# Two chained transformer blocks on one core: other order of the first loads, and planner costs of instructions fitted to a trace

## Chip, cores and metric

One core of one Trainium2 chip. The metric is the device time of one execution in microseconds (us): the kernel before takes 3340.11 us, the median of 3 runs (3338.27 to 3342.55).

## The reference, cut to what matters

The input x is 512 tokens by 1024 features in fp32. Two blocks of depth two follow each other:

```python
# first block
x = x + even_mixer(rmsnorm(x))       # gated linear attention (GLA), 4 heads, and differential attention, 4 heads
x = x + conv_ffn(rmsnorm(x))         # 1024 -> 2 x 2816 -> 1024, causal convolution of 3
x = x + odd_mixer(rmsnorm(x))        # dilated attention, 3 patterns
x = x + conv_ffn(rmsnorm(x))
# second block, for i in (0, 1); cs is a context of 256 tokens, needed for i == 0 only
m = silu(c) @ w_mod[i] + b_mod[i]    # 9 x 1024 modulation values, w_mod is 1024 x 9216; likewise from c_ctx
x = x + 0.5 * m2 * swiglu(modulate(x, m0, m1))
x = x + m5 * mixer(modulate(x, m3, m4))   # i == 0: attention of 8 query heads on 2 key heads, and pooling; i == 1: gated mixing
x = x + 0.5 * m8 * swiglu(modulate(x, m6, m7))
```

In the even mixer the eight head outputs are normed (the GLA heads are also multiplied by silu of a gate), joined to 1024 features and multiplied by `w_out`.

## The kernel before

**Numbers.** Every large product is done as three matmuls of a rounded fp32 type (hi·hi, hi·lo, lo·hi; `mm3`). Activations stand as pairs: `hh`, `hl` for a normed input, `mh`, `ml` for the middle tiles that go into an output projection. A weight block of 128 rows by 1024 columns (512 KB, `raw`) comes by one DMA, mostly from SP's queue (`wdma`), and is split into `whi` on ACT and `wlo` on DVE, each in two halves of 512.

**Stages.** They run one after the other: a0 (even mixer), b0 (FFN), a1 (odd mixer), b1, c0 (half FFN, with the context), d0 (attention and pooling), e0, c1, d1, e1. Tokens are worked on in one piece of 512 columns, or in two halves of 256 at the first and the last projection of a stage (`passes`), so that the next norm can begin on the first half.

**The order.** Each engine runs its instructions in program order. The program order is made when the kernel is built: small steps of a stage (a head's scores, its norm, a softmax) are generators, called tasks, and after every `mm3` the method `tick` may step some of them. It asks a planner: `Clock` keeps a modelled time for each engine, `Clock.cost` gives the duration it assumes for an instruction, and a task is stepped when its inputs are due by the modelled time of TensorE. Only the first `width` tasks whose predecessors are done are looked at (4 in a0 and a1, 8 in d0). The same model decides when weights are split ahead (`wahead`) and when a step of `mod_task` is taken. So a change of a number in `Clock.cost` reorders instructions in the whole program, on all engines, while the work stays what it is.

**a0's end.** The projection out of the mixer is in two parts. `proj_out` takes the four heads of the differential attention, 96 matmuls of 512 columns into tiles `gm`, while the GLA runs: decays (`la` on PE, `lae` on ACT, `lc` on DVE), running sums (`cum`, `cul`), scores (`attp`), states (`kv`), outputs (`oa`). Then `o_norm` norms the head outputs: a square on ACT (`osq`), a sum over the features on PE (`ss`), on DVE `hv`, on ACT a logarithm and an exponential (`rb`), on DVE five operations of 512 columns (two write `osq`, three write `rb`), then `mh` on ACT and `ml` on DVE. `final` multiplies the four GLA heads by their part of `w_out`, 256 columns at a time. The gates need silu (`sg`), which stands in another table of ACT than the logarithm and the exponential, so a change between them is an `ACT_TABLE_LOAD`.

**d0's attention.** 16 units (`attn_unit`): eight score matmuls into three PSUM tiles (`as1` twice 512 columns, `as0` 2 x 256), row maxima on DVE (`amx`, `nb`), four exponentials with sums on ACT (`ap1`, `ap0`), twelve transposes on PE (`at`), copies (`aw`), 25 matmuls with the values (`apo`), and a scaling (`arb`, `ao`).

**The modulation.** `mod_task` multiplies `w_mod` by silu(c) row block by row block on DVE, into sums `macc`, with 512 KB loads `rawm`; its steps are spread over a0 to c0.

**Recording.** In the profile every instruction of the engines carries line 172, that of the wrapper that records it. Tile names with a number behind (`gm_2828`) are single buffers; the trace leaves the number out.

Of the kernel before, what the change touches and what calls it, by code (L numbers as in the profile page):

```python
# [9 lines left out]
F32 = mybir.dt.float32  # L10
# [5 lines left out]
OP = mybir.AluOpType  # L16
# [12 lines left out]
NG = 66  # L29
# [68 lines left out]
class Clock:  # L98
# [18 lines left out]
    def cost(self, engine, op, out, ins, extra):  # L117
        n = 1
        for x in (out if op != "tensor_reduce" else ins[0]).shape[1:]:
            n *= x  # L120
        if engine == "tensor":
            if op == "transpose":
                return 0.11
            dt = ins[-1].dtype
            if dt == F32:
                return max(0.213, n / 600)
            return n / 2400 if dt == BF16 or n >= 256 else n / 600
        if op == "dma_start":
            return 0.06
        psum = any(x.space == PSUM for x in ins)  # L130
        if engine == "vector":
            scalars = op in ("tensor_scalar", "scalar_tensor_tensor")
            each = 0.00052 if op == "tensor_scalar" and not psum else 0.00833 if op == "reciprocal" else 0.00104
            return (0.13 if scalars else 0.07) + 0.03 * psum + each * n
        if engine == "scalar":
            return 0.1 + 0.00083 * n + 0.05 * sum(len(x.shape) == 2 and x.shape[1] == 1 for x in ins[1:]) + extra
        return 0.1 + 0.0023 * n

    def issue(self, engine, op, args, kwargs):
# [5 lines left out]
        end = start + self.cost(engine, op, out, ins, 0.24 * ("accum_out" in kwargs))  # L145
# [36 lines left out]
class Kern:  # L182
    def __init__(self, tc, ctx, a, out, dump=None, plan=None):
# [701 lines left out]
    def mod_task(self):  # L885
        nc = self.nc
        parts = [(i, u, k0) for i in range(2) for u in range(36) for k0 in range(0, NK, KU)]
        raws = []

        def load(j):  # L890
            if j < len(parts):
                i, u, k0 = parts[j]
                raw = self.wp.tile([P, KU, 256], F32, tag="rawm", name="rawm", bufs=MB)
                nc.sync.dma_start(raw, self.a["w_mod"][i, u, :, k0:k0 + KU])
                raws.append(raw)
# [3 lines left out]
        rows = [self.sp.tile([P, 96], F32, tag="mrow", name="mrow", bufs=3) for _ in range(2)]  # L899
# [11 lines left out]
        for j, (i, u, k0) in enumerate(parts):  # L911
            if k0 == 0:
                todo = [(self.sc, self.mT[i])]
                if i == 0 and u < 20:
                    todo.append((self.scc, self.mcT))
                accs = [self.wp.tile([P, 256], F32, tag="macc", name="macc", bufs=2) for _ in todo]
# [12 lines left out]
            if k0 + KU == NK:  # L929
                x = u % 12  # L930
                for acc, r in zip(accs, rows):
                    nc.vector.transpose(tr := self.wp.tile([P, 256], F32, tag="mtr", name="mtr", bufs=1), acc)
                    nc.vector.tensor_reduce(r[:, 8 * x:8 * x + 8], tr.rearrange("p (b c) -> p b c", c=32),
                                            axis=AX.X, op=OP.add)
                last = len(todo) == 2 and u == 19
                if x == 11 or last:
                    yield
                    for (_, m), r in list(zip(todo, rows))[1 if last else 0:]:
                        sums(i, m, r, u - x, x + 1)
                    if x == 11:  # L940
                        self.mod_done = 36 * i + u
                        rows = [self.sp.tile([P, 96], F32, tag="mrow", name="mrow", bufs=3) for _ in range(2)]
                yield
# [610 lines left out]
    def attn_unit(self, t, c, qs, kk, va, ao):  # L1554
# [257 lines left out]
def lay_out(inputs):  # L1812
# [4 lines left out]
    def blocks(w, cols=None):  # L1817
# [4 lines left out]
        return con(w.reshape(k // P, P, m // 256, 256).transpose(2, 1, 0, 3))  # L1822
# [27 lines left out]
    d["w_mod"] = np.stack([blocks(x) for x in f("w_mod_2")])  # L1850
# [79 lines left out]
```

## Time and profile before

| what | value |
|---|---|
| median of 3 runs | 3340.11 us |
| the profiled execution | 3336.78 us, its span 3335.0 us |
| PE (TensorE) busy | 3290.2 us, 99% |
| PEld (weight loads of PE) busy | 2874.7 us, 86% |
| DVE (VectorE) busy | 2101.9 us, 63% |
| ACT (ScalarE) busy | 1237.7 us, 37% |
| DMA | 355.73 MB, mean 107 GB/s |

PE is busy nearly all the time, so what it waits for, and where, says more than the shares do. A row of the timeline has start, duration, engine, line, operation, output<-inputs, shapes and count, and in brackets the idle time before and what ended it. A row of the waits has the engine and what it was about to run, whom it waited for, microseconds in total, times and the longest. The clock of PE has two levels, 1.2 and 2.4 GHz, written as 0.50 and 1.00 in the windows.

### The profile page before, as it was taken

The page shows a single profiled execution, that of the slowest core. Times are in us where ns is not written, and L with a number is a line of the kernel's source. Part 1 is how long each engine was busy: PE and PEld are TensorE (multiplying, and loading weights), DVE is VectorE, ACT ScalarE, POOL GpSimd, SP SyncE. Part 2 cuts the span into 40 slices and gives each one's busy share as a digit, 9 for nine tenths or more (in the row PEclk, how much of TensorE's full clock was granted, in tenths as well). Part 3 has the DMA queues.
Part 4 walks back from the last instruction along what each step waited for, and adds up shares of the span by engine and source line. Part 5 has one row for each costly group of instructions (what it writes and reads, how often), then busy time and mean ns, then how long its engine had stood idle before and what let it go on. Part 6 is the DMA issues. An engine that isn't in the chain of part 4 may idle for free.

```text
span 3335.0 us, 48346 instructions
## 1 busy us (share of the span) xinstructions
PE 3290.2 (99%) x19172; PEld 2874.7 (86%) x19172; DVE 2101.9 (63%) x4577; ACT 1237.7 (37%) x2515; POOL 5.2 (0%) x13
## 2 busy tenths in 40 slices
PE   8999999999999999999999989999999999999999
PEld 7789888988998889888888977988898889998888
DVE  6868988857498878655555776855663335463333
ACT  4544434364443434212222465322332233442231
POOL 0000000000000000000000000000000000000000
PEclk9999999999999999999999999999999999999999
DMA  3223444322134443443333301445522233232232
GB/s 120 70 64 105 150 125 137 122 65 76 58 114 145 127 133 107 142 146 119 112 118 126 96 24 51 148 137 158 160 93 82 95 103 99 87 98 91 92 101 70
DMA packets 105814, 355.73 MB, mean 107 GB/s; under 512 B 12642, under 2 KB 18931, under 8 KB 105587
## 3 DMA queue, kind: packets, MB, share of 16 engines
q1 hardware_dynamic: 105154, 351.98, 33.5%
q8 instruction: 150, 2.46, 0.3%
q14 instruction: 78, 0.63, 0.1%
q10 hardware_dynamic: 432, 0.66, 0.1%
HBM read 350.50 MB, written 2.10 MB: 106 GB/s over the span
## 4 chain that ended last, share of the span: by engine, by line
PE 90%; DVE 7%; ACT 2%; issue 1%; DMA 1%; SPq 0%; DVEq 0%; ACTq 0%
PE gm L172 81%; PE gt L172 4%; ACT ap L172 1%; DVE wlo L172 1%; PE ss L172 1%; DVE nt L172 1%; DVE amx L172 1%; DVE x L172 0%; PE os L172 0%; PE opo L172 0%; DVE rb L172 0%; DVE rs_t L172 0%; DVE nsq L172 0%; PE qst L172 0%; DVE hl L172 0%
## 5 line engine op out<-in xcount | busy, mean ns | idle before, releaser
L172 PE MATMUL gm<-hh,whi 128*128 128x512 f32 (+1 forms) x2872 | 1040.4, 362 | 6.9 <-ACT whi L172 6.9
L172 PE MATMUL gm<-hl,whi 128*128 128x512 f32 (+1 forms) x2872 | 1033.9, 360 | 5.6 <-DVE hl L172 5.6
L172 PE MATMUL gm<-hh,wlo 128*128 128x512 f32 (+1 forms) x2872 | 1031.5, 359 | 5.1 <-DVE wlo L172 5.1
L172 DVE TENSOR_TENSOR wlo<-raw,whi 128x512 fp32r<-128x512 f32 (+1 forms) x1028 | 662.1, 681 | 77.2 <-ACT whi L172 75.2
L172 ACT ACTIVATE whi<-raw 128x512 fp32r<-128x512 f32 (+1 forms) x1028 | 582.4, 617 | 296.6 <-DMA raw<-in_ffn_w_dram 106.5
L172 PEld LDWEIGHTS gm<-hh,wlo 128*128 128x128 f32 x2872 | 543.7, 189 | 88.5 <-DVE wlo L172 5.9
L172 PEld LDWEIGHTS gm<-hh,whi 128*128 128x128 f32 x2872 | 544.6, 190 | 74.0 <-ACT whi L172 6.9
L172 PEld LDWEIGHTS gm<-hl,whi 128*128 128x128 f32 x2872 | 544.5, 190 | 72.9 <-DVE hl L172 6.6
L172 PE MATMUL gm<-mh,whi 128*128 128x512 f32 (+1 forms) x1696 | 576.6, 340 | 0.0
L172 PE MATMUL gm<-ml,whi 128*128 128x512 f32 (+1 forms) x1696 | 573.0, 338 | 0.8 <-DVE ml L172 0.8
L172 PE MATMUL gm<-mh,wlo 128*128 128x512 f32 (+1 forms) x1696 | 571.7, 337 | 0.0
L172 DVE TENSOR_TENSOR ga<-ga,gm 128x512 f32<-128x512 f32 (+1 forms) x110 | 68.0, 633 | 497.7 <-PE gm L172 328.2
L172 PEld LDWEIGHTS gm<-mh,wlo 128*128 128x128 f32 x1696 | 321.8, 190 | 34.7
L172 PEld LDWEIGHTS gm<-ml,whi 128*128 128x128 f32 x1696 | 322.2, 190 | 29.1 <-DVE ml L172 1.0
L172 PEld LDWEIGHTS gm<-mh,whi 128*128 128x128 f32 x1696 | 322.2, 190 | 28.9 <-issue 0.9
L172 ACT ACTIVATE ga<-gm 128x512 f32<-128x512 f32 (+1 forms) x110 | 58.8, 554 | 716.6 <-PE gm L172 716.6
L172 DVE SCALAR_TENSOR_TENSOR macc<-rawm,sc,macc 128x256 f32<-128x256 f32 x504 | 244.0, 484 | 15.4
L172 DVE SCALAR_TENSOR_TENSOR x<-gm,modt,x 128x256 f32<-128x256 f32 (+1 forms) x184 | 105.9, 607 | 226.4 <-PE gm L172 226.3
L172 PEld LDWEIGHTS gm<-hc,whi 128*128 128x128 f32 x736 | 135.0, 188 | 29.0 <-ACT whi L172 1.6
L172 DVE SCALAR_TENSOR_TENSOR cy<-gm,vec,cy 128x511 f32<-128x511 f32 (+1 forms) x176 | 127.7, 746 | 45.9 <-ACT cy L172 42.8
L172 PE MATMUL gm<-hc,whi 128*128 128x256 f32 x736 | 145.1, 281 | 1.3 <-ACT whi L172 1.3
L172 ACT ACTIVATE nsq<-x 128x256 f32<-128x256 f32 x160 | 60.2, 414 | 176.8 <-DVE x L172 176.7
(314 smaller groups left out, 3425.6 us busy)
## 6 DMA issues: line engine op xcount, KB each, us to landing
raw<-in_ffn_w_dram SPq DMA_DIRECT2D x256, 512.0 KB, 4.4
rawm<-in_w_mod_dram SPq DMA_DIRECT2D x144, 512.0 KB, 4.4
raw<-in_ffn_w_up_dram SPq DMA_DIRECT2D x88, 512.0 KB, 3.8
raw<-in_ffn_w_down_dram SPq DMA_DIRECT2D x40, 512.0 KB, 3.7
raw<-in_od_w_in_dram SPq DMA_DIRECT2D x36, 512.0 KB, 3.8
raw<-in_ev_w_in_dram SPq DMA_DIRECT2D x23, 512.0 KB, 3.7
raw<-in_w_in_c_dram SPq DMA_DIRECT2D x16, 512.0 KB, 4.3
raw<-in_w_in_a_dram SPq DMA_DIRECT2D x10, 512.0 KB, 4.4
```

The source lines that it names most:

```text
L172: return f(*args, **kwargs)
```

## The change

Three things are edited.

- The first loads: of the four first weight blocks one more is issued ahead of the second half of x on SP's queue, and one goes to ACT's queue, ahead of the constants.
- `Clock.cost` gets other numbers for matmuls, DVE and ACT; `NG`, the number of 2 KB work tiles per partition, goes from 66 to 64.
- Two pieces of work are cut differently. `mod_task` takes 1024 columns with one DVE instruction (144 parts, of 512 KB each as before) in the place of four of 256. `attn_unit` does all row maxima of a unit first, three reductions and two small operations, and then the four exponentials; before, each half had its maxima and then its exponentials.

The core of the diff:

```diff
-NG = 66
+NG = 64
...
-            dt = ins[-1].dtype
-            if dt == F32:
-                return max(0.213, n / 600)
-            return n / 2400 if dt == BF16 or n >= 256 else n / 600
+            if ins[-1].dtype == F32:
+                rows, cols = ins[0].shape[0], ins[0].shape[-1]
+                return max(0.214, n / 597) * (0.6 if rows <= 64 or cols <= 64 else 1.0)
+            return (n + 32) / 2400 if n >= 256 else 0.066
...
-            scalars = op in ("tensor_scalar", "scalar_tensor_tensor")
-            each = 0.00052 if op == "tensor_scalar" and not psum else 0.00833 if op == "reciprocal" else 0.00104
-            return (0.13 if scalars else 0.07) + 0.03 * psum + each * n
+            fast = not psum and op in ("tensor_scalar", "tensor_copy")
+            each = 0.00052 if fast else 0.00833 if op == "reciprocal" else 0.00104
+            return 0.155 + 0.06 * (scalars > 0) + each * n
         if engine == "scalar":
-            return 0.1 + 0.00083 * n + 0.05 * sum(len(x.shape) == 2 and x.shape[1] == 1 for x in ins[1:]) + extra
+            return 0.2 + 0.00083 * n + 0.075 * scalars + extra
...
-            self.wdma()
+            self.wdma()
+            self.wdma(nc.scalar)
+            self.wdma()
         load(0, 4, 1)
         nc.scalar.dma_start(self.cst[:, :256], a["cst"][:, :256])
         load(4, 8, 1)
-        if plan is not None:
-            for _ in range(2):
-                self.wdma()
...
-                for k in range(KU):
-                    sk = s[:, k0 + k:k0 + k + 1]
-                    if k0 + k == 0:
-                        nc.vector.tensor_scalar(acc, raw[:, k], sk, None, op0=OP.mult)
-                    else:
-                        nc.vector.scalar_tensor_tensor(acc, raw[:, k], sk, acc, op0=OP.mult, op1=OP.add)
+                sk = s[:, k:k + 1]
+                if k == 0:
+                    nc.vector.tensor_scalar(acc, raw, sk, None, op0=OP.mult)
+                else:
+                    nc.vector.scalar_tensor_tensor(acc, raw, sk, acc, op0=OP.mult, op1=OP.add)
...
+        for j in range(2):
+            nc.vector.tensor_reduce(mx[:, j:j + 1], s1[j], axis=AX.X, op=OP.max)
+        nc.vector.tensor_reduce(mx[:, 2:4], s0.rearrange("p (j k) -> p j k", j=2), axis=AX.X, op=OP.max)
+        nc.vector.tensor_tensor(nb, mx[:, 0:2], mx[:, 2:4], op=OP.max)
+        nc.vector.tensor_mul(nb, nb, neg[:, 2 * t:2 * t + 2])
         for j in range(2):
             k, half, cc = slice(j, j + 1), slice(j * C, (j + 1) * C), slice(2 * t + j, 2 * t + j + 1)
-            nc.vector.tensor_reduce(mx[:, k], s1[j], axis=AX.X, op=OP.max)
-            nc.vector.tensor_reduce(mx[:, 2 + j:3 + j], s0[:, half], axis=AX.X, op=OP.max)
-            nc.vector.scalar_tensor_tensor(nb[:, k], mx[:, k], mx[:, 2 + j:3 + j], neg[:, cc], op0=OP.max, op1=OP.mult)
```

The counts of instructions: PE has the same 18483 matmuls and transposes before and after, in another order; DVE goes from 4574 to 4006; ACT has 14 table loads in the place of 10, the four new ones in a0.

**Where the order moves.** A row is an instruction as the program has it, with its tiles. Line 172 of the kernel before is line 173 of the changed one.

SP's queue at the start of the program, before (`raw` are weight blocks, `x` the input; the second block of weights is `raw_84` in both):

```order
L172 DMA raw_84<-in_ev_w_in_dram 128x1024
L172 DMA x_75<-in_xT_dram 128x4x256 x2
L172 DMA raw_89<-in_ev_w_in_dram 128x1024
L172 DMA raw_91<-in_ev_w_in_dram 128x1024
L172 DMA vec_77<-in_vec_dram 128x600
L172 DMA cst_76<-in_cst_dram 128x1042
```

and after, where the third block, `raw_86`, has gone to ACT's queue, just behind the first:

```order
L173 DMA raw_84<-in_ev_w_in_dram 128x1024
L173 DMA raw_88<-in_ev_w_in_dram 128x1024
L173 DMA x_75<-in_xT_dram 128x4x256 x2
L173 DMA vec_77<-in_vec_dram 128x600
L173 DMA cst_76<-in_cst_dram 128x1042
L173 DMA raw_128<-in_ev_w_in_dram 128x1024
```

Two blocks stand ahead of the second half of x (`128x4x256`) on SP, and one on ACT, where one stood on SP and none on ACT beside the first.

PE at a0's end, before: the four sums `ss` of the GLA heads' norms, and what stands behind them. `mh_1692`, `mh_1976` are heads of the differential attention, long done; 81 such rows of `proj_out` follow the last `ss` before the first row of `final`, which reads `mh_2665`, the first GLA head:

```order
L172 MATMUL ss_2632<-osq_2615,cst_76 128x512
L172 MATMUL ss_2639<-osq_2617,cst_76 128x512
L172 MATMUL ss_2646<-osq_2619,cst_76 128x512
L172 MATMUL ss_2653<-osq_2621,cst_76 128x512
L172 MATMUL gm_2624<-mh_1692,whi_2228 128x512
L172 MATMUL gm_2624<-ml_1693,whi_2228 128x512
L172 MATMUL gm_2624<-mh_1692,wlo_2229 128x512
```

and after: `mh_2796` and `ml_2797` are the first GLA head, so these are the rows of `final`, right behind the last `ss`; all 96 matmuls of `proj_out` stand further up, between the steps of the GLA:

```order
L173 MATMUL ss_2763<-osq_2755,cst_76 128x512
L173 MATMUL ss_2770<-osq_2757,cst_76 128x512
L173 MATMUL ss_2777<-osq_2759,cst_76 128x512
L173 MATMUL ss_2784<-osq_2761,cst_76 128x512
L173 MATMUL gm_2828<-mh_2796,whi_2405 128x256
L173 MATMUL gm_2828<-ml_2797,whi_2405 128x256
L173 MATMUL gm_2828<-mh_2796,wlo_2406 128x256
```

On DVE, `ml_2797` comes after the five operations of all four heads, as `ml_2666` does in the kernel before.

ACT in the last third of a0, before: the decays of the second pair of GLA heads (`lae_2083`), and the square `osq_2125` of the last head of the differential attention; the gates `sg` come 20 rows later:

```order
L172 ACTIVATE lae_2083<-la_2079 128x512
L172 ACTIVATE lae_2083<-lae_2083 128x512 x2
L172 ACTIVATE dor_1119<-po_2088 128x128
L172 ACTIVATE whi_2109<-raw_1783 128x512
L172 ACTIVATE osq_2125<-dor_1119 128x512
L172 ACTIVATE rb_2131<-hv_2129 128x512
L172 ACTIVATE rb_2131<-rb_2131 128x512
```

and after: the decays of the first pair (`lae_2293`), the gates of two heads, the same head's square (here `osq_2331`), with three table loads between them:

```order
L173 ACT_TABLE_LOAD
L173 ACTIVATE lae_2293<-lae_2293 128x512
L173 ACTIVATE dor_1113<-po_2305 128x128
L173 ACT_TABLE_LOAD
L173 ACTIVATE sg_2320<-sg_2320 128x512
L173 ACTIVATE sg_2323<-sg_2323 128x512
L173 ACT_TABLE_LOAD
L173 ACTIVATE osq_2331<-dor_1113 128x512
L173 ACTIVATE rb_2337<-hv_2335 128x512
L173 ACTIVATE rb_2337<-rb_2337 128x512
```

PE's sum over that head is `ss_2333<-osq_2331`; the matmuls ahead of it on PE are those of `gm_2195` and `gm_2196`, which the gates `sg_2320` and `sg_2323` are made from. Behind `ss_2333` stand the second `la`, nine matmuls of `proj_out` for three heads of the differential attention, and then one that reads `mh_2354`, this same head.

DVE in one of the last units of d0's attention, before:

```order
L172 TENSOR_REDUCE amx_20773<-as1_20763 128x1
L172 TENSOR_REDUCE amx_20773<-as0_20762 128x1
L172 SCALAR_TENSOR_TENSOR nb_20774<-amx_20773,neg_20205 128x1
L172 TENSOR_REDUCE amx_20773<-as1_20764 128x1
L172 TENSOR_REDUCE amx_20773<-as0_20762 128x1
L172 SCALAR_TENSOR_TENSOR nb_20774<-amx_20773,neg_20205 128x1
```

and after, one unit:

```order
L173 TENSOR_REDUCE amx_20160<-as1_20150 128x1
L173 TENSOR_REDUCE amx_20160<-as1_20151 128x1
L173 TENSOR_REDUCE amx_20160<-as0_20149 128x2
L173 TENSOR_TENSOR nb_20161<-amx_20160 128x2
L173 TENSOR_TENSOR nb_20161<-nb_20161,neg_19626 128x2
```

The second half's maxima no longer stand behind those of the first half. On PE, no projection matmul stands between the scores of the last nine units in the changed program; before, 69 matmuls of 512 columns stand there.

## Rows read from the trace of the kernel before

**Rows 1.** The page's head: span, and busy time of the engines.

```profile
span 3335.0 us, 48346 instructions
PE 3290.2 (99%) x19172; PEld 2874.7 (86%) x19172; DVE 2101.9 (63%) x4577; ACT 1237.7 (37%) x2515; POOL 5.2 (0%) x13
```

**Rows 2.** Windows: us from:to, length, busy time by engine, PE clock, DMA.

```profile
16.68:21.30 4.62, 4.62 (x21) 4.62 (x22) 4.62 (x10) 4.62 (x12) 2.20 (x4) 0.50 0.64 201
...
1938.00:2067.00 129.00, 113.98 (x902) 95.08 (x901) 90.26 (x246) 80.43 (x208) 0.00 (x0) 0.97 0.12 40
1979.40:1984.00 4.60, 4.49 (x22) 4.49 (x23) 3.65 (x12) 1.24 (x3) 0.00 (x0) 0.51 0.00 0
```

**Rows 3.** Timeline of the start: ACT, DVE and PE around PE's longest early wait.

```profile
14.06 0.63 ACT L172 ACTIVATE whi<-raw 128x512 fp32r<-128x512 f32 x1 [1.66 <-DMA raw<-in_ev_w_in_dram]
...
15.33 0.69 DVE L172 TENSOR_TENSOR nsq<-nsq 128x512 f32<-128x512 f32 x1 [3.03 <-ACT nsq L172]
...
16.68 0.58 PE L172 MATMUL gm<-hh,wlo 128*128 128x256 f32 x1 [4.41 <-DVE wlo L172]
```

**Rows 4.** Timeline of a0's end, PE and DVE: last `ss` to `final`.

```profile
233.41 0.79 PE L172 MATMUL gm<-mh,whi 128*128 128x512 f32 x1
...
234.62 0.68 DVE L172 TENSOR_TENSOR osq<-rb 128x512 f32<-128x512 f32 x1
...
238.79 0.68 DVE L172 TENSOR_TENSOR osq<-rb 128x512 f32<-128x512 f32 x1
...
249.42 0.75 DVE L172 SCALAR_TENSOR_TENSOR rb<-rb,vec,sg 128x512 f32<-128x512 f32 x1
...
250.69 0.68 DVE L172 TENSOR_TENSOR ml<-rb,mh 128x512 fp32r<-128x512 f32 x1
...
252.22 0.28 PE L172 MATMUL gm<-mh,whi 128*128 128x256 f32 x1
```

**Rows 5.** Timeline of ACT in a0: decays, table loads, gates.

```profile
168.31 1.29 ACT L172 ACTIVATE lae<-lae 128x512 f32<-128x512 f32 x2
...
199.90 1.28 ACT L172 ACT_TABLE_LOAD   x1
201.24 1.23 ACT L172 ACTIVATE sg<-sg 128x512 f32<-128x512 f32 x2
...
250.86 1.28 ACT L172 ACT_TABLE_LOAD   x1
252.15 1.15 ACT L172 ACTIVATE whi<-raw 128x512 fp32r<-128x512 f32 x2
```

**Rows 6.** Timeline of one head's norm in a0, DVE's five operations: first and last.

```profile
162.15 0.68 DVE L172 TENSOR_TENSOR osq<-rb 128x512 f32<-128x512 f32 x1
...
165.04 0.49 DVE L172 TENSOR_SCALAR rb<-rb,vec 128x512 f32<-128x512 f32 x1
```

**Rows 7.** Waits of PE from 90 to 300 us, a0's second half and b0's start.

```profile
PE gm L172 <- DVE hl L172: 3.4, 2, 1.9
PE gm L172 <- DVE ml L172: 0.8, 1, 0.8
```

**Rows 8.** Waits of PE from 1935 to 2070 us, d0's attention: the longest.

```profile
PE qst L172 <- ACT qsq L172: 6.5, 1, 6.5
```

**Rows 9.** Groups by shape, 1938 to 2067 us: maxima on DVE, exponentials on ACT.

```profile
L172 ACT ACTIVATE ap<-as,nb,cc 128x512 f32<-128x512 f32 x32 | 24.9, 778 | 34.9 <-DVE nb L172 34.9
...
L172 DVE TENSOR_REDUCE amx<-as 128x1 f32<-128x512 f32 x32 | 21.9, 683 | 0.6 <-PE as L172 0.6
...
L172 ACT ACTIVATE ap<-as,nb,cc 128x256 f32<-128x256 f32 x32 | 17.8, 555 | 0.0
L172 ACT ACTIVATE aw<-at 128x512 f32<-128x512 f32 x32 | 17.4, 607 | 3.9 <-PE at L172 3.9
...
L172 DVE TENSOR_REDUCE amx<-as 128x1 f32<-128x256 f32 x32 | 13.4, 420 | 18.2 <-ACT ap L172 17.9 <-PE as L172 0.2
```

**Rows 10.** Timeline of PE in the attention: one unit's value products and transposes.

```profile
1951.30 1.53 PE L172 MATMUL apo<-aw,va 128*64 128x128 f32 x24
1952.76 1.53 PE L172 MATMUL at<-cst,ap 128*128 128x128 f32 x12
```

**Rows 11.** Groups by shape, 40 to 2200 us: the modulation's products on DVE.

```profile
L172 DVE SCALAR_TENSOR_TENSOR macc<-rawm,sc,macc 128x256 f32<-128x256 f32 x423 | 204.8, 484 | 13.0
```

More of the change, by code (lines that the diff above doesn't have):

```diff
@@ L130, in cost @@
         psum = any(x.space == PSUM for x in ins)
+        scalars = sum(len(x.shape) == 2 and x.shape[1] == 1 for x in ins[1:])
         if engine == "vector":
-            scalars = op in ("tensor_scalar", "scalar_tensor_tensor")
-            each = 0.00052 if op == "tensor_scalar" and not psum else 0.00833 if op == "reciprocal" else 0.00104
-            return (0.13 if scalars else 0.07) + 0.03 * psum + each * n
+            fast = not psum and op in ("tensor_scalar", "tensor_copy")
+            each = 0.00052 if fast else 0.00833 if op == "reciprocal" else 0.00104
+            return 0.155 + 0.06 * (scalars > 0) + each * n
         if engine == "scalar":
-            return 0.1 + 0.00083 * n + 0.05 * sum(len(x.shape) == 2 and x.shape[1] == 1 for x in ins[1:]) + extra
+            return 0.2 + 0.00083 * n + 0.075 * scalars + extra
         return 0.1 + 0.0023 * n
@@ L144, in issue @@
         start = max([self.t[engine]] + [self.done(x, engine) for x in ins + [out]])
-        end = start + self.cost(engine, op, out, ins, 0.24 * ("accum_out" in kwargs))
+        end = start + self.cost(engine, op, out, ins, 0.2 * ("accum_out" in kwargs))
         self.t[engine] = end
@@ L886, in mod_task @@
         nc = self.nc
-        parts = [(i, u, k0) for i in range(2) for u in range(36) for k0 in range(0, NK, KU)]
+        parts = [(i, u, k) for i in range(2) for u in range(9) for k in range(NK)]
         raws = []
@@ L891, in load @@
             if j < len(parts):
[L892 to L894 removed]
+                i, u, k = parts[j]
+                raw = self.wp.tile([P, D], F32, tag="rawm", name="rawm", bufs=MB)
+                nc.sync.dma_start(raw, self.a["w_mod"][i, u, :, k])
                 raws.append(raw)
@@ L898, in mod_task @@
             load(j)
-        rows = [self.sp.tile([P, 96], F32, tag="mrow", name="mrow", bufs=3) for _ in range(2)]
+        new_rows = lambda: [self.sp.tile([P, 96], F32, tag="mrow", name="mrow", bufs=3) for _ in range(2)]
+        rows = new_rows()
         def sums(i, m, r, u0, n):
@@ L909, in sums @@
                                      self.v("b_mod", i * 72 + 2 * u0, 2 * n)[rr])
-        for j, (i, u, k0) in enumerate(parts):
-            if k0 == 0:
+        for j, (i, u, k) in enumerate(parts):
+            if k == 0:
                 todo = [(self.sc, self.mT[i])]
-                if i == 0 and u < 20:
+                if i == 0 and u < 5:
                     todo.append((self.scc, self.mcT))
-                accs = [self.wp.tile([P, 256], F32, tag="macc", name="macc", bufs=2) for _ in todo]
+                accs = [self.wp.tile([P, D], F32, tag="macc", name="macc", bufs=2) for _ in todo]
             raw = raws.pop(0)
             for (s, m), acc in zip(todo, accs):
-                for k in range(KU):
-                    sk = s[:, k0 + k:k0 + k + 1]
-                    if k0 + k == 0:
-                        nc.vector.tensor_scalar(acc, raw[:, k], sk, None, op0=OP.mult)
-                    else:
-                        nc.vector.scalar_tensor_tensor(acc, raw[:, k], sk, acc, op0=OP.mult, op1=OP.add)
+                sk = s[:, k:k + 1]
+                if k == 0:
+                    nc.vector.tensor_scalar(acc, raw, sk, None, op0=OP.mult)
+                else:
+                    nc.vector.scalar_tensor_tensor(acc, raw, sk, acc, op0=OP.mult, op1=OP.add)
                 if len(todo) == 2 and acc is accs[0]:
@@ L928, in mod_task @@
             yield
-            if k0 + KU == NK:
-                x = u % 12
+            if k + 1 < NK:
+                continue
+            for v in range(4):
+                uu = 4 * u + v
+                x = uu % 12
                 for acc, r in zip(accs, rows):
-                    nc.vector.transpose(tr := self.wp.tile([P, 256], F32, tag="mtr", name="mtr", bufs=1), acc)
+                    nc.vector.transpose(tr := self.wp.tile([P, 256], F32, tag="mtr", name="mtr", bufs=1),
+                                        acc[:, v * 256:(v + 1) * 256])
                     nc.vector.tensor_reduce(r[:, 8 * x:8 * x + 8], tr.rearrange("p (b c) -> p b c", c=32),
                                             axis=AX.X, op=OP.add)
-                last = len(todo) == 2 and u == 19
+                last = len(todo) == 2 and uu == 19
                 if x == 11 or last:
@@ L938, in mod_task @@
                     for (_, m), r in list(zip(todo, rows))[1 if last else 0:]:
-                        sums(i, m, r, u - x, x + 1)
+                        sums(i, m, r, uu - x, x + 1)
                     if x == 11:
-                        self.mod_done = 36 * i + u
-                        rows = [self.sp.tile([P, 96], F32, tag="mrow", name="mrow", bufs=3) for _ in range(2)]
+                        self.mod_done = 36 * i + uu
+                        rows = new_rows()
                 yield
@@ L1815, in lay_out, with blocks @@
     con = np.ascontiguousarray
-    def blocks(w, cols=None):
+    def blocks(w, cols=None, n=256):
         if cols is not None:
@@ L1821, in blocks @@
         k, m = w.shape
[L1822 removed]
+        return con(w.reshape(k // P, P, m // n, n).transpose(2, 1, 0, 3))
     def pm(v):
@@ L1849, in lay_out @@
     d["ffn_w2"] = np.stack([np.stack([blocks(x) for x in y]) for y in f("ffn_w2_2")])
-    d["w_mod"] = np.stack([blocks(x) for x in f("w_mod_2")])
+    d["w_mod"] = np.stack([blocks(x, n=D) for x in f("w_mod_2")])
     hcols = lambda h: np.arange(h * 64, (h + 1) * 64)
```

## The prediction

> **What bounds the kernel now.** I read the page's head first: PE is busy for 3290.2 of 3335.0 us, DVE for 2101.9, ACT for 1237.7 [rows 1]. The change leaves PE's 18483 instructions as they are and only reorders them, so it can win at most what PE loses: 44.8 us of idle time, and the stretches in which its clock stands at the lower level. It can lose any amount, since a wait of PE is added to the end in full. So I went by the waits of PE and, in each place, compared the order before and after: what PE has to do (its cover) between the instruction that starts a chain on ACT and DVE and the one that needs the chain's result. DVE's 568 fewer instructions count only where such a chain runs on DVE.
>
> PE loses its time in few places. In the attention of d0 it is busy for 113.98 of 129.0 us, so 15.0 us are lost there [rows 2], 6.5 of them in one wait for the squares of a query [rows 8]. At the start it waits 4.41 us [rows 3]. At a0's end and the start of b0 it waits 3.4 for the normed input `hl` and 0.8 for `ml` [rows 7]. After the wait of 4.41 us, and after that of 6.5 us, the clock was at its lower level, 1.2 GHz, for 4.6 us each time (0.50 and 0.51 granted) [rows 2]; at half speed that is 2.3 us of work lost each time.
>
> **The change, part by part.**
>
> *The first loads.* PE's wait of 4.41 us ends when DVE has split a weight; DVE does a sum of squares before that (15.33 us), whose second pair of squares stands on ACT behind the split of the third weight, which waited for its DMA until 14.06 us [rows 3]. The third weight now lands earlier, but the second half of x lands later: the first half (1024 KB), four weight blocks of 512, 128 KB of constants and the first 512 of its own are 3712 KB, as many as came up to the third weight's end before (three blocks and all of x). On ACT an `hh` of that half stands ahead of both pairs of squares and of the split, and the order there is unchanged. So x arrives at about 14.1 us, and ACT then has an `hh`, two pairs of squares and a split to do, where before a split and one pair stood behind the late weight: PE goes on about 1 us later (an `hh` and a pair are 1.2 by estimate). Bounds: the wait vanishes with its clock loss (-4.4 - 2.3 = -6.7), or x comes 1.5 us later still (+2.5). I take **+1.0**.
>
> *a0's second half.* This is the term that decides. Four waits arise or grow.
>
> First, `final`. Before, the last `ss` is followed by 81 matmuls of `proj_out`, from 233.41 to 252.22 us: 18.8 us of cover. In that time DVE does the norms: the five operations of the first head begin at 234.62, those of the next at 238.79, the last ends at 250.17, and `ml` ends at 251.37 [rows 4]. PE waits 0.8 for it [rows 7]. After, nothing stands between the last `ss` and `final`, whose second matmul needs `ml_2797`, and DVE comes to that only after all 20 operations of the four heads. From rows 4 the four heads take 250.17 - 234.62 = 15.55 us, less two foreign operations of 0.6 in between, and one of 0.6 goes before `ml` too; 14.3 + 0.7 for `ml` + 0.6 from the last `ss` to the first operation gives 15.6 us. PE has no other work: +15.6 - 0.8 = **+14.8**. Bounds 13 and 17, as two small operations may go before.
>
> Second, `ss_2333`. The matmuls ahead of it end the tiles that the gates are made from. From there: DVE's two products of 0.7, ACT's two silus, of which the second ends about 2.1 us in if ACT is free, a table load of 1.28, the square of 0.63 [rows 5]: 4.1 us, and ACT comes to the silus 0.5 later, since two more table loads and three `lae` stand before them. I take **+4.3** (bounds 2 and 6).
>
> Third, the matmul that reads `mh_2354`. After `ss_2333` PE has nine matmuls of 0.23 = 2.1 us of cover. The chain is `hv` 0.7, two `rb` 1.3, three `lae` 1.9, `lc` 0.7, DVE's five operations 3.4 (162.15 to 165.53 [rows 6]), `mh` 0.63, `ml` 0.7: 9.3 us (an activation of this size is 0.63 each [rows 5]). +9.3 - 2.1 = **+7.2** (bounds 4 and 9).
>
> Fourth, the outputs `oa` and the squares behind them stand together with no cover: **+1.5** by estimate (0 to 3). The clock: after the third and the first of these waits I count 2.2 us each, as after the two long waits before [rows 2]: **+4.4** (0 to 6.6). On the other side, the norm behind a0 has 54 matmuls of cover in the place of 24, 3.6 us by 0.12 each, and so the waits for `hl` go: **-3.4** [rows 7]. Together **+28.8**, with bounds at +12 and +38.
>
> ACT loads its table four times more, all in this stretch, 1.28 us each, and in the row at 250.86 the next activation begins 0.01 us after the load's end [rows 5]. Three of the loads are in the second wait and counted there. The Trainium skill, *ScalarE: Activation LUTs*, section "What ACT_TABLE_LOAD costs", puts a change of table at 1.28 us and a drain of 1.38 behind that, and advises doing all of one table's functions before the next, which speaks against this order. The rows show the 1.28 and no drain beyond it; by the page's sum the second wait would be some 4 us longer, and the time 3369.
>
> *d0's attention.* A unit had four maxima and two `nb` on DVE; the 256-column maximum waited for the first exponential, 17.9 us in all over 32 [rows 9], so about 0.6 each. Now three reductions of 0.68 and two small operations, 2.4 us, come first, and the four exponentials follow without a gap: 2 x 1.33 = 2.7 us (778 and 555 ns [rows 9]). That takes the inner waits away and shortens ACT's and DVE's part. But the last nine units have no projection matmul beside them. There PE has per unit eight score matmuls (1.4), 1.3 for the transposes and 1.5 + 0.2 for the value products [rows 10], 4.4 us, while a unit's maxima (2.4), exponentials (2.7) and copies (0.6 [rows 9], then the scaling, 0.6 by estimate) follow each other through the same PSUM tiles: 6.3 us. Six units at 1.9 are 11.4 us of new waits, and one for a query's squares of about 3.7 remains in the place of 6.5. So some 15 of idle time against 15.0 + 2.3 before: **-3**. Bounds: everything is covered (-14), or nine units pay 1.9 to 2.3 and the query's wait stays (+6).
>
> *The modulation.* 423 products of 256 columns on DVE cost 484 ns each [rows 11]; one of 1024 in the place of four saves the fixed part. DVE isn't what PE waits for there, and loads are of the same number and size. A longer operation, 1.3 us by estimate, can stand before a split that PE needs. **0** (-3 to +3). All other stretches (b0, a1, b1, c0, e0 to e1): the numbers of matmuls between the starts of a norm and its use differ by up to 18 of 120, in both directions: **0** (-5 to +4).
>
> **The sum.** 1.0 + 28.8 - 3 = +26.8; since the middle values of a0's second and third wait can overlap (ACT works ahead while PE stands), I take 2 off: **+25**. The profiled execution took 3336.78, so it would take 3361.8; it lies 3.3 below the median, and against that the changed kernel takes 3340.1 + 25 = **3365 us**.
>
> **The rivals.**
>
> *Attention wins (faster).* Place: d0, 1938 to 2067 us. If the copies and maxima of neighbouring units overlap in the tail, PE is bound by its own 113.98 us and all 15.0 + 2.3 go. For it: the wait on the inner exponential is 17.9 us of DVE's idle time [rows 9]. Against it: the empty tail. By itself it gives -17.3; it decides the sign if a0 costs less than 10, which takes a `final` that doesn't wait for all four heads. With a0 at +8 and the start at +1: 3332.
>
> *Nothing to measure.* a0 at its lower bound of +12, attention at -10, the start as it is: +2, 3342.
>
> *The attention's tail is worse.* If a unit's scores wait until the unit before has been copied out, nine units pay 3 us more each than now: +10 in the place of -3, and a0 at +30: +41, 3381.
>
> *The change doesn't do what it says:* excluded, the order shows the moved rows.
>
> **How the numbers follow.** Forecast (a0 between 20 and 34, attention between -10 and +5): 0.68. Attention wins: 0.10. Nothing to measure: 0.12. Worse tail: 0.10. A measurement of this kernel tells 0.2%, 6.7 us, from no change: so faster 0.10, same 0.12, slower 0.78. The range leaves out the faster case and the worst: from 3338 (start and attention at their lower bounds, a0 at 16) to 3380 (a0 at 36, attention at +3).
>
> **What would show it.** In the changed profile: a wait of PE `gm` for DVE `ml` of about 15 us just ahead of `final` in a0, one of about 7 for the same some 30 us earlier, one of `ss` for ACT `osq` of about 4; the waits for `hl` behind a0 gone; PE's waits in the attention of 12 to 16 us, most in the last six units, on ACT `ap` or DVE; PE's busy time as before but for the clock. It is wrong if `final` finds `ml` ready, or if a0's chain runs ahead of PE because PE is later there than I think.

## The result

The changed kernel takes 3373.57 us (median of 4 runs, 3371.87 to 3375.12), the kernel before 3339.89 beside it: a ratio of 1.0101, with a 95% interval of 1.0089 to 1.0112. It is 33.7 us slower; 25 were forecast (3365), and the range went to 3380. In the profiled executions the spans are 3370.1 and 3335.0 us, 35.1 apart, and the sums below are made against these.

The page of the changed kernel (busy time of the engines; against [rows 1]):

```profile
PE 3301.0 (98%) x19172; PEld 2885.9 (86%) x19172; DVE 1982.9 (59%) x4009; ACT 1246.0 (37%) x2519; POOL 5.4 (0%) x13
```

DVE gave back 119 us and the kernel became slower all the same. PE is busy for 10.8 us more with the same instructions, most of it time at the lower clock (the windows below), and idle for 24.3 us more.

**Where the time went.** Each half of a norm has two small matmuls `nbc` on PE, so their starts serve as milestones. The kernel before, timeline of PE: the first norm behind a0, the last ahead of d0's attention, and one behind the stage that follows it:

```profile
274.04 0.49 PE L172 MATMUL nbc<-cst,rs_y 128*128 128x128 f32 x3
1880.82 0.49 PE L172 MATMUL nbc<-cst,rs_y 128*128 128x128 f32 x3
2444.86 0.60 PE L172 MATMUL nbc<-cst,rs_y 128*128 128x128 f32 x4
```

The changed kernel, the same three:

```profile
302.42 0.38 PE L173 MATMUL nbc<-cst,rs_y 128*128 128x128 f32 x2
1910.15 0.49 PE L173 MATMUL nbc<-cst,rs_y 128*128 128x128 f32 x3
2480.42 0.49 PE L173 MATMUL nbc<-cst,rs_y 128*128 128x128 f32 x3
```

The changed kernel is 28.4 us behind at the end of a0, 29.3 at d0, 35.6 after d0 and e0, and 35.1 at the end (the spans). So nearly all of it is lost in two places: 28 us in a0, and 6 in d0's attention and the norm behind it. From b0 to c0, 1600 us in which nearly everything was reordered too, the lag grows by 1 us.

**a0.** Waits of PE from 90 to 310 us in the changed kernel (against [rows 7]):

```profile
PE gm L173 <- DVE ml L173: 10.1, 1, 10.1
PE gm L173 <- ACT mh L173: 7.6, 2, 5.0
PE ss L173 <- ACT osq L173: 7.3, 2, 6.3
```

All waits that were forecast are there, and the 3.4 us for `hl` are gone. Of the two waits for `osq`, the one of 1.0 us is that behind the outputs `oa`, for which 1.5 were forecast. The waits for `ss_2333` and `mh_2354`, with what lies between them:

```profile
209.49 2.08 PE L173 MATMUL ss<-osq,cst 128*128 128x512 f32 x2 [6.29 <-ACT osq L173]
211.50 2.07 PE L173 MATMUL la<-wa,ar 17*128 17x256 f32 x4
...
220.27 0.80 PE L173 MATMUL gm<-mh,whi 128*128 128x512 f32 x1 [2.56 <-ACT mh L173]
```

The timeline of PE and DVE ahead of `final`, against [rows 4]:

```profile
266.78 1.45 PE L173 MATMUL ss<-osq,cst 128*128 128x512 f32 x3
273.23 0.58 PE L173 MATMUL gm<-mh,whi 128*128 128x256 f32 x1 [5.01 <-ACT mh L173]
283.87 0.58 PE L173 MATMUL gm<-ml,whi 128*128 128x256 f32 x1 [10.06 <-DVE ml L173]
...
268.87 0.68 DVE L173 TENSOR_TENSOR osq<-rb 128x512 f32<-128x512 f32 x1
...
283.13 2.49 DVE L173 TENSOR_TENSOR ml<-rb,mh 128x512 fp32r<-128x512 f32 x4
```

DVE works from 268.87 to 283.13 on the four heads without a gap (20 operations in 14.3 us), `ml` follows, and PE does one matmul in those 15 us.

**d0.** The longest waits of PE from 1960 to 2120 us in the changed kernel (against [rows 8]):

```profile
PE qst L173 <- ACT qsq L173: 5.4, 1, 5.4
PE as L173 <- ACT ap L173: 5.3, 5, 2.3
```

Behind that, from 2100 to 2140 us:

```profile
PE gm L173 <- DVE hl L173: 3.3, 2, 1.9
```

In the kernel before, this wait behind the attention is 0.7. Windows of the changed kernel (from:to, length, busy time by engine, PE clock, DMA): the attention against [rows 2], two short stretches at the lower clock in its tail, then a0 from its first norm to the norm behind it, and the two stretches at the lower clock in a0:

```profile
1955.00:2100.00 145.00, 129.65 (x989) 110.86 (x989) 95.64 (x247) 85.44 (x215) 0.00 (x0) 0.95 0.07 21
2062.39:2065.80 3.41, 2.92 (x11) 2.74 (x12) 2.79 (x9) 3.41 (x11) 0.00 (x0) 0.50 0.00 0
2076.04:2079.45 3.41, 3.41 (x19) 3.08 (x20) 2.41 (x7) 0.90 (x3) 0.00 (x0) 0.50 0.00 0
29.53:302.42 272.89, 245.81 (x1577) 202.71 (x1576) 177.84 (x439) 122.30 (x273) 2.10 (x4) 0.93 0.20 61
205.53:226.01 20.48, 13.96 (x32) 9.11 (x33) 7.98 (x15) 8.68 (x14) 1.57 (x3) 0.50 0.09 26
270.39:287.45 17.06, 4.16 (x17) 3.87 (x18) 16.34 (x25) 6.30 (x10) 0.00 (x0) 0.50 0.00 0
```

The same stretch of a0 in the kernel before:

```profile
29.13:274.04 244.91, 241.69 (x1607) 200.97 (x1606) 177.65 (x441) 116.24 (x270) 1.99 (x4) 1.00 0.22 68
```

15.4 us are idle in the attention, as many as before (15.0), and the clock is lower: 0.95 where it was 0.97. In a0 the idle time goes from 3.2 to 27.1 us, and 18.1 us of PE's work (13.96 + 4.16) run at 0.50, where none did; if half of that is lost, it is some 9 us by estimate.

### The profile page after: what moved, and what is told of

It reads as the page before. It is cut to its first block, busy times and chain, and to the rows that moved or that the text cites. A ratio compares the mean times of both kernels' runs of the same rounds, so it can differ in the third digit from the quotient of the medians.

```text
span 3370.1 us, 47802 instructions
## 1 busy us (share of the span) xinstructions
PE 3301.0 (98%) x19172; PEld 2885.9 (86%) x19172; DVE 1982.9 (59%) x4009; ACT 1246.0 (37%) x2519; POOL 5.4 (0%) x13
## 4 chain that ended last, share of the span: by engine, by line
PE 93%; DVE 4%; ACT 2%; issue 0%; DMA 0%; DVEq 0%; ACTq 0%
PE gm L173 83%; PE gt L173 4%; ACT ap L173 1%; PE ss L173 1%; DVE amx L173 1%; PE os L173 0%; PE qst L173 0%; DVE wlo L173 0%; PE ds L173 0%; DVE rb L173 0%; DVE nt L173 0%; PE opo L173 0%; DMA x<-in_xT_dram 0%; PE at L173 0%; PE oa L173 0%
## 5 line engine op out<-in xcount | busy, mean ns | idle before, releaser
L173 PE MATMUL gm<-ml,whi 128*128 128x512 f32 (+1 forms) x1696 | 575.3, 339 | 10.1 <-DVE ml L173 10.1
L173 PEld LDWEIGHTS gm<-ml,whi 128*128 128x128 f32 x1696 | 323.8, 191 | 38.6 <-DVE ml L173 10.8
L173 DVE SCALAR_TENSOR_TENSOR macc<-rawm,sc,macc 128x1024 f32<-128x1024 f32 x126 | 161.2, 1279 | 12.3 <-DMA rawm<-in_w_mod_dram 12.3
L173 PEld LDWEIGHTS gm<-hc,whi 128*128 128x128 f32 x736 | 136.7, 191 | 27.5
L173 ACT ACTIVATE cy<-gm,vec 128x512 f32<-128x512 f32 x88 | 64.2, 780 | 167.8 <-PE gm L173 167.8
```

The costliest lines, as they stand in the source:

```text
L173: return f(*args, **kwargs)
```

## The experiments

Theory: the planner's new numbers alone make the loss, since they start the GLA's chain later against PE's work, and PE runs out of cover. The rivals are the recut work, the loads, and an ACT or DVE that is late as such.

**1. The new numbers alone.** The kernel before with the edits of `Clock.cost` and the 0.2 for `accum_out`:

```diff
-            return 0.1 + 0.00083 * n + 0.05 * sum(len(x.shape) == 2 and x.shape[1] == 1 for x in ins[1:]) + extra
+            return 0.2 + 0.00083 * n + 0.075 * scalars + extra
...
```

> The kernel before with the planner's new numbers as the only edit (old loads, old modulation, old attention unit, 66 work tiles). Theory (the new numbers alone move a0's instructions so that final finds no cover): the loss of 29 us up to a0's end is there in full, the waits of PE for osq, mh and ml in a0 as in the changed kernel (6, 2.5 and 15 us together for final), and the attention of d0 loses too, as the old unit has no shorter chain: 3375 us (3369 to 3383). Rival (the loss comes from the first loads or from the recut work, the numbers only add small shifts): 3340 us (3335 to 3348), with final waiting about 1 us.

3374.05 us, ratio 1.0100 (1.0085 to 1.0115), span 3372.2. Waits of PE in a0:

```profile
PE gm L173 <- DVE ml L173: 10.1, 1, 10.1
PE gm L173 <- ACT mh L173: 8.3, 2, 5.0
PE ss L173 <- ACT osq L173: 7.3, 2, 6.3
```

The same waits, but for 0.7 us more at `mh`: the whole loss, without new loads, modulation or attention unit.

**2. Everything but the new numbers.** The other half of the diff (loads, modulation, attention unit, 64 tiles).

> The changed kernel with the planner's old numbers: new loads, new modulation, new attention unit, 64 work tiles. Theory: a0 is as in the kernel before (final waits about 1 us for ml, no wait for osq), and the new attention unit, with projection matmuls between all but the last four units, gains 3 to 10 us of the 17 lost there: 3334 us (3329 to 3341). Rival (the recut work makes the loss): over 3360 us.

3337.09 us, ratio 0.9990 (0.9981 to 1.0000). a0 is that of the kernel before. But the gain of 3 to 10 us in the attention isn't there; the longest waits from 1935 to 2075 us:

```profile
PE qst L172 <- ACT qsq L172: 5.0, 2, 4.6
PE as L172 <- ACT ap L172: 4.3, 5, 1.3
```

So the recut work isn't the cause of the loss. It is worth 2.5 us by the medians, and 0 to 6 by the interval; the time lies in the range that was expected, but not by way of the attention, so that half of the theory fell, and the last three runs take it up.

**3 and 4. The old numbers in a0; in a0, c0 and d0.** The changed kernel with both sets of numbers:

```diff
+            self.clock.old = name in ("a0",)            # run 4: ("a0", "c0", "d0")
             step()
```

> The changed kernel, but the planner takes the old numbers while it orders a0 and the new ones from b0 on. Theory: the 29 us of a0 go, the 6 us of d0 stay: 3345 us (3341 to 3350). Rival (a0's waits are only where a loss that the new numbers make everywhere becomes visible, and come back later): 3360 us or more.

> As the run before, with the old numbers in c0 and d0 as well. Theory (the order of the attention's tail, nine units without a projection matmul beside them, costs what the shorter unit gains): against the run before another 8 us go (5 to 14), half in the attention, 2 to 3 in the waits for hl behind it: 3337 us (3331 to 3342). Rival (the new unit itself is slower): no difference to the run before, 3345.

3347.88 us (ratio 1.0022, 1.0013 to 1.0032) and 3336.78 (0.9993, 0.9984 to 1.0003). The first lacks 25.7 us of the loss and the second another 11.1. In the first, the longest wait of PE from 90 to 310 us is the 3.4 us for `hl`, as before, while the longest from 1860 to 2140 us is that of the changed kernel:

```profile
PE qst L197 <- ACT qsq L197: 5.4, 1, 5.4
```

So the losses in a0 and in d0 are separate, and neither comes back later. c0 was switched together with d0, so the 11.1 us are not split between the two; they are more than the milestones give to d0, and the spans of the two profiled executions differ by 7.4 (3344.8 and 3337.4). The second run is as fast as run 2, which has the old numbers everywhere: in b0, a1, b1 and from e0 on the new numbers cost nothing that shows.

**5. The table loads.** In the changed kernel the gates' function is replaced, with no other effect on the order:

```diff
-                nc.scalar.activation(t, t, AF.Silu)
+                nc.scalar.activation(t, t, AF.Exp)
```

> The changed kernel with the exponential in the place of silu for the four gates of a0 (another function, so the gates' values differ; the planner sees the same cost, and PE's order is that of the changed kernel). Five table loads of a0 go. Theory (ss waits for the last head's square because three table loads stand ahead of it on ACT): that wait falls from 6.3 to 2.5 to 3.5 us, what is left being DVE's two products, the activations and the square; the other waits of a0 stay within 1 us: 3370 us, 3 to 4 less than the changed kernel. Rival (ACT is late there for other work, the loads fill its idle time): the wait stays at 5 us or more.

One run, 3372.99 us. ACT ahead of the square, first in the changed kernel, then in this one:

```profile
200.51 0.60 ACT L173 ACTIVATE lae<-la 128x512 f32<-128x512 f32 x1
...
201.79 1.28 ACT L173 ACT_TABLE_LOAD   x1
203.08 0.63 ACT L173 ACTIVATE lae<-lae 128x512 f32<-128x512 f32 x1
...
203.90 1.28 ACT L173 ACT_TABLE_LOAD   x1
206.27 1.23 ACT L173 ACTIVATE sg<-sg 128x512 f32<-128x512 f32 x2 [1.09 <-DVE sg L173]
207.52 1.28 ACT L173 ACT_TABLE_LOAD   x1
208.81 0.63 ACT L173 ACTIVATE osq<-dor 128x512 f32<-128x512 f32 x1
```

```profile
199.75 0.60 ACT L173 ACTIVATE lae<-la 128x512 f32<-128x512 f32 x1 [0.47 <-PE la L173]
...
204.23 1.23 ACT L173 ACTIVATE sg<-sg 128x512 f32<-128x512 f32 x2 [1.74 <-DVE sg L173]
205.47 1.28 ACT L173 ACT_TABLE_LOAD   x1
206.77 0.63 ACT L173 ACTIVATE osq<-dor 128x512 f32<-128x512 f32 x1
```

DVE in the changed kernel, at the decays:

```profile
203.75 0.69 DVE L173 SCALAR_TENSOR_TENSOR lc<-la,lae 128x512 f32<-128x512 f32 x1 [4.36 <-ACT lae L173]
```

The wait of `ss` falls from 6.3 to 3.9, not as far as expected (2.5 to 3.5), and a0's end comes 1.8 us earlier. The time is not 3 to 4 us below the changed kernel's: this one run lies among that kernel's own four (3371.87 to 3375.12).

Two of the three loads go, but only one of them was on the path to PE. From the first decay to the square ACT takes 8.30 us in the changed kernel (200.51 to 208.81) and 7.02 here (199.75 to 206.77): 1.28 less. That is the load among the decays: `lc` stands ahead of the gates' products on DVE and waits 4.36 us for the decays, so that load reaches PE by way of DVE. Behind the second load ACT waited 1.09 us for DVE in any case, so it was hidden. The rest of the gain comes from loads further ahead (at 191.49 and 193.44 us of the changed kernel, ahead of another head's `rb`): without them the decays begin earlier.

The section of the Trainium skill that the prediction draws on ("What ACT_TABLE_LOAD costs" in *ScalarE: Activation LUTs*) would give 2.66 us for that one load with its drain (the advice on the order stands in the page's next section, "Table sets: the hidden batching unit"). The trace doesn't agree: the activation that follows a load begins 0.01 to 0.02 us after it, and the path lost 1.28, so here it is the load alone.

**6. The cover put back.** In the changed kernel, half of `proj_out` is written behind the heads' norms:

```diff
-        self.proj_out("ev_w_out", None, [ob[i] for i in range(4)], first=4)
+        self.proj_out("ev_w_out", None, [ob[i] for i in range(4)], first=4, blocks=(0, 1))
         self.finish(gn)
+        self.proj_out("ev_w_out", None, [ob[i] for i in range(4)], first=4, blocks=(2, 3))
```

> The changed kernel, where half of proj_out (48 of 96 matmuls of 512 columns, 10.9 us) is written behind the GLA heads' norms, just ahead of final; the planner keeps the new numbers. Theory (final waits since it has no cover): the wait of 15.1 us for mh and ml falls to 2 to 5 us, and the 40 us before it, in which the GLA's steps were all covered, get 3 to 9 us of new waits, since 48 matmuls less stand there: 3366 us (3360 to 3372). Rival (DVE and ACT themselves are late by then, cover or not): final waits over 10 us still.

One run, 3371.05 us. PE at the sums, and a window ahead of them, in which PE did the GLA's outputs `oa` and its first sums `ss`:

```profile
269.96 3.49 PE L173 MATMUL ss<-osq,cst 128*128 128x512 f32 x4 [7.19 <-ACT osq L173]
```

```profile
245.71:262.78 17.07, 17.05 (x80) 12.75 (x80) 4.28 (x9) 6.09 (x18) 0.00 (x0) 0.50 0.00 0
```

The wait at `final` is gone altogether (2 to 5 us were expected to stay), and still a0's end lies 27.9 us behind the kernel before instead of 28.4. Counted from a0's first norm, which comes 1.4 us later in this execution than in the changed kernel's, a0 is 1.9 us shorter. The GLA's chain, now bare, makes PE wait 7.2 us ahead of the sums, and PE's idle time between the two norms falls only from 27.1 to 19.7 us. Most of these 7.4 us come back as work at the lower clock: from 245.71 to 262.78 PE has no gap and works at 0.50, while in the changed kernel, with `proj_out` among the GLA's small matmuls, the clock was 0.99 from 225 to 262. So half of the 15 us moved up the chain as a wait, and a third turned into lower clock. That refines the theory: what a0 lacks isn't matmuls at one place but matmuls after the chain's start. Counted in PE's large matmuls (0.227 us for 512 columns, 0.12 for 256), the chain's first `la` stands behind 107 us of work in the kernel before and behind 138 in the changed one, so some 30 us less are left to cover it (in the traces it starts at 166.5 and 198.2 us).

**7. Part of the numbers.** The kernel before with ACT's new numbers only (the line shown at run 1, with the count of scalars written out, and the 0.2):

> The kernel before with only ACT's numbers of the new planner costs. In its order the sums of the GLA heads stand in two pairs, 12 matmuls of proj_out between them and none behind the second. Theory (the wait of final is DVE's 15.6 us from the first ss, less the cover): 15.6 - 2.7 - 1.2 for the second pair = 11 to 12 us of wait at final, about 13 us more than the kernel before: 3353 us (3349 to 3358). Rival (it takes all of the new numbers to make the loss): 3342 or less.

One run, 3348.28 us, just below the range; a0's end is 10.1 us behind where 13 were expected, and the rival's 3342 is not met either. Waits of PE there:

```profile
PE gm L172 <- DVE ml L172: 8.4, 2, 5.5
PE gm L172 <- ACT mh L172: 2.8, 2, 2.2
```

11.2 us at `final`, as the length of the chain less its cover gave. The first `la` stands behind 124 us of work: of these three orders, the later the chain starts, the larger the loss. ACT's numbers alone so make a third of a0's loss; those of DVE and of the matmuls were not tried by themselves.

**8. The chain first.** The changed kernel with all new numbers, and the GLA's tasks at the head of the planner's list:

```diff
-        la = self.spawn(self.log_decay(ar, gs))
+        la = self.spawn(self.log_decay(ar, gs), front=True)
...
-        gl = self.spawn(self.gla(gs), [la])
+        gl = self.spawn(self.gla(gs), [la], front=True)
```

> The changed kernel with all its new numbers, where the decays and the GLA's steps are put at the head of the planner's list, ahead of the steps of the differential attention; no other edit. In its order the first running sums stand 12 matmuls of 256 columns behind a0's last token projection, 75 matmuls of proj_out stand behind the last ss, and the last head of the differential attention is normed just before the outputs of the GLA. Theory, as the run with the cover put back left it (the loss is that the GLA's chain starts some 30 us of PE's work later, wherever proj_out stands): final waits 0 to 1 us, 17 us of cover against a chain of 15.6; the wait for the last differential head's mh stays and is 4 to 7 us: 3354 us (3347 to 3361). Rival (what is late is DVE and ACT in a0 as a whole, so that another chain is late in its place): 3364 or more.

3355.86 us, ratio 1.0051 (1.0034 to 1.0068): 17.7 less than the changed kernel. Waits of PE in a0:

```profile
PE dt L173 <- DVE dp L173: 5.7, 1, 5.7
PE gm L173 <- DVE ml L173: 2.9, 2, 2.7
```

The time is the one expected and the waits are half so: `final` waits 2.7 and not 15 (0 to 1 was expected), but the long wait is now one of the differential attention, for `dp`, whose chain became the late one, as in the rival, though the time isn't the rival's 3364. The GLA's chain starts at 108.9 us here, 58 us ahead of the kernel before, and a0's end is still 12.9 us behind (`nbc` at 286.91). So an early start of the one chain takes back more than half of a0's loss with DVE's and ACT's work unchanged; it isn't all that decides, since another chain then lacks cover.

**9. The modulation alone.** The kernel before with pieces of 1024 columns (and 64 tiles, which they need):

> The kernel before with 64 work tiles and the modulation in pieces of 1024 columns, nothing else. Theory (DVE's time is covered there): DVE is busy for 115 to 125 us less, and the time is that of the kernel before within 4 us, 3336 to 3344. Rival (the 1.28 us operations hold up splits of weights): over 3346.

One run, 3337.49 us. The page:

```profile
PE 3292.4 (99%) x19172; PEld 2877.2 (86%) x19172; DVE 1985.6 (60%) x4025; ACT 1240.3 (37%) x2515; POOL 4.8 (0%) x13
```

116 us of DVE less, and no difference in time. (In the kernel before the products run from 306 to 2429 us, from b0 to e0, and not from a0 to c0, as the text ahead of the prediction has it.)

**10 to 12. Queries first.** In d0 the second pair of queries is projected ahead of the pooling's second half; on the kernel of run 2, twice, and on the kernel before:

```diff
-        pools(1, self.gemm_m(w(4), NK, h))
         query(1, self.gemm_m(w(1), NK, h))
+        pools(1, self.gemm_m(w(4), NK, h))
```

> The changed kernel with the planner's old numbers (as the second run), and in d0 the projection for the second pair of queries ahead of that for the second half of the pooling. Theory (of the attention's 17 us some 7 are one chain: the query's square on ACT behind four exponentials, with 15 matmuls of cover on PE, and the lower clock behind the wait): the waits for the squares (5.0 us) and the clock's loss go, the rest of the attention stays within 3 us: 3331 us (3326 to 3336). Rival (the stretch is bound by a unit's chain on DVE and ACT, and a wait that is taken away comes back in the tail): 3335 to 3340.

> The kernel before, with the projection for the second pair of queries ahead of that for the second half of the pooling as the only edit: old unit, old modulation, old loads, old numbers. Theory (the gain of the earlier run with this order comes from the queries' squares, and the shorter unit alone gained nothing): 3336 us (3331 to 3339), no wait of qst over 1 us. Rival (it takes the shorter unit for it): 3340 or more.

> The fastest kernel so far once more, beside the run before on one chip: new loads, new modulation, new attention unit, 64 work tiles, old numbers, queries first. Theory: 3334 us (3331 to 3337) as before, 1 to 3 us faster than the kernel with the old unit, since the inner wait of a unit is gone. Rival (the unit is worth nothing in any order): the two within 1 us.

On the kernel of run 2: 3334.07 us, ratio 0.9981 (0.9972 to 0.9991), and again 3334.25, 0.9980 (0.9971 to 0.9989). That is 6 us faster than the kernel before and 39 faster than the changed one. On the kernel before: 3344.66, ratio 1.0010 (1.0002 to 1.0019). The waits of PE from 1935 to 2070 us, with the new unit (run 12), and from 1935 to 2075 with the old one (run 11), the longest:

```profile
PE as L172 <- ACT ap L172: 6.3, 5, 3.9
PE at L172 <- ACT ap L172: 1.9, 3, 0.7
```

```profile
PE as L172 <- ACT ap L172: 7.0, 5, 2.9
PE at L172 <- ACT ap L172: 4.7, 3, 1.7
```

The wait for the query's square is gone in both, but the theory that the gain comes from it fell: with the old unit 3336 us were expected, and PE waits for the units' exponentials instead (7.0 and 4.7 us; 1.5 each in the kernel before). The groups by shape show the unit: DVE's smaller maximum waited 18.1 us for `ap` with the old one, and the exponentials 46.0 us for `nb`; 27.5 with the new one.

```profile
L172 DVE TENSOR_REDUCE amx<-as 128x1 f32<-128x256 f32 x32 | 13.5, 421 | 18.2 <-ACT ap L172 18.1
L172 ACT ACTIVATE ap<-as,nb,cc 128x512 f32<-128x512 f32 x32 | 24.9, 778 | 46.1 <-DVE nb L172 46.0
```

```profile
L172 ACT ACTIVATE ap<-as,nb,cc 128x512 f32<-128x512 f32 x32 | 25.1, 784 | 27.6 <-DVE nb L172 27.5
```

So, by two pairs (run 2 against the kernel before, run 12 against run 11), the shorter unit pays only when the units' chain is what PE waits for. The two kernels differ by 10.4 us, where 1 to 3 were expected. Loads and modulation differ too, and the loads alone were not tried. But in the traces the two are 3.3 us apart at the last norm ahead of d0's attention (`nbc` at 1882.82 and 1879.50) and 13.0 at the first behind it (2092.46 and 2079.46), with the same work done, so most of it arises in the attention.

## Why the prediction was right, and where it was off

- **Direction and place: right.** a0 was forecast at +28.8 and is 28.4 behind at its end; runs 1 and 3 show that the numbers' order of a0 makes it. That the sum is so close is partly luck: the waits were forecast to add 27.8 us and added 23.9 (3.2 to 27.1), the clock 4.4 and some 9, and the two errors cancel. The whole, 25 forecast and 33.7 measured, is short mainly by the attention, the norm behind it and the 2 us taken off for an overlap, which had no basis. The range's lower end, 3338, isn't the sum of the bounds it names either: -6.7, -14 and +16 give 3335.
- **`final`: right.** 15.6 us were summed from [rows 4], 15.1 measured (5.0 for `mh`, 10.1 for `ml`).
- **`ss_2333`: mis-sized,** 4.3 against 6.3. I had ACT's queue ahead of it but not DVE's: `lc` waits there for the decays, ahead of the gates' products (run 5), and the decays themselves start late behind earlier loads.
- **The matmul on `mh_2354`: mis-sized,** 7.2 against 2.6. The chain was about right: 8.7 us from the end of `ss` at 211.6 to 220.27. The cover was taken as nine matmuls at full speed, 2.1 us. The second `la` (2.07 us) lies ahead of them, and PE ran at the lower clock, so that from 211.6 to 217.7 us it had 6.1 us to do.
- **The clock: right behind the two waits, too small in all.** 4.4 were forecast, 2.2 behind each wait. From 220.27 to 226.01 PE worked 5.7 us at 0.50, which costs some 2.9, and the 4.16 us at 0.50 around `final`'s waits cost some 2.1. The clock was low already ahead of the wait that ended at 220.27, from 209.49 to 217.7; the 4 us that this costs mostly fill what would have been waiting time.
- **The norm behind a0: right,** the 3.4 us are gone. The same step was left out in d0: there the matmuls between the norm's end and its use fall from 54 to 30, and the wait for `hl` grows from 0.7 to 3.3 us. I had put the "other stretches" at 0.
- **The attention: wrong by its sign,** -3 against some +3.7 in the stretch itself (35.6 less 29.3, and less the 2.6 just named). The idle time is as summed (15.1 forecast, 15.4), its parts less so: the query's wait is 5.4 for 3.7, the waits from 2060 us on add up to 8.3 for 11.4. The sign comes from the clock: I let its loss of 2.3 go with a shorter wait for the query, but the wait stayed long, and two more stretches at 0.50 came in the tail (0.95 in the window, 0.97 before). The rival that the tail is much worse didn't come; the one that the attention wins shows only in runs 10 and 12, in another order.
- **Loads and modulation: right,** 0.4 us behind at the first norm (1.0 forecast; the second half of x arrives at 13.8 us where 14.1 was worked out), and nothing for 116 us of DVE in run 9. The loads by themselves were not tried.

## What to carry to other kernels

Where PE is nearly always busy, an order is read by its cover: count the matmuls between the instruction that starts a chain on other engines and the one that needs its result, and compare that with the chain's length from the trace. Cover moved from one place to another of the same chain gained 2 of 28 us here (run 6); starting the chain earlier gained 17.7 (run 8), until another chain lacked cover. Numbers that are fitted to a trace don't by themselves make a greedy planner's plan better, so the order has to be looked at after each refit. Why the planner starts the GLA later by the new numbers was not followed up.

## What the hardware showed unexpectedly

In the changed kernel PE's clock was granted 0.50 from 205.53 to 226.01 us, around the end of the wait of 6.3 us, with sums and projections of 512 columns, small matmuls and a further wait of 2.6 us in it; behind the longer wait of 15 us, work without gaps began at 283.87, and the clock was low until 287.45. It doesn't take a long wait: in run 6 PE was busy for 17.05 of 17.07 us from 245.71 on, granted 0.50, mostly with the GLA's small matmuls, and the waits ahead of it were 0.36 and 0.68 us. What brings the level down there is not shown.
